# Mixer block: later turns for solves, bonus products and transposes, some elementwise work moved from GpSimd to VectorE, memory values in two bank pairs, no zeroing products

## The chip, the cores and the metric

The program runs on one core of a Trainium2 chip. The metric is the device time of one execution in microseconds (us); of several runs the median counts. The engines are named as in the profile: PE is TensorE (PEld its weight loads), DVE is VectorE, ACT is ScalarE, POOL is GpSimd, SP is SyncE, whose queue issues the DMAs.

## What is computed

Two layers run on 512 positions of width 1024. The first adds a mixer (retention heads beside RWKV-7 heads), a cross-attention over 256 memory rows and an MLP; the second is a gated attention layer. The change touches the mixer and the preparation of the memory keys and values. The parts of the reference that matter:

```python
def wkv7_scan(r, w, k, v, a_vec, b_vec):
    def step(state, inp):
        r_t, w_t, k_t, v_t, a_t, b_t = inp
        sa = jnp.einsum('bhvk,bhk->bhv', state, a_t)
        state = (state * w_t[:, :, None, :] + sa[..., None] * b_t[:, :, None, :]
                 + v_t[..., None] * k_t[:, :, None, :])
        return state, jnp.einsum('bhvk,bhk->bhv', state, r_t)

# in rwkv7_mixer:
    kk = kk / jnp.maximum(jnp.sqrt(jnp.sum(jnp.square(kk), axis=-1, keepdims=True)), 1e-12)
    k = k * (1.0 + (a - 1.0) * k_a)                      # the key update
    y = wkv7_scan(..., -kk, kk * ah)
    bonus = jnp.sum(rh * kh * r_k, axis=-1, keepdims=True) * vh

# in first_block, with memory_cross_attention:
    x = x + y @ w_out[l]
    k, v = jnp.split(rmsnorm(mem, norm_mem[l]) @ w_kv, 2, axis=-1)
```

## The kernel before

**Products in three parts.** A weight unit of 128x1024 is loaded to `raw`, rounded by ACT into a high part `wh` (L291) and subtracted into a low part `wl` (L292, `pump`). A product with an activation is high x high, high x low and low x high (`mm3`, `tile_t`, `quad`). `lowpart` (L246) says which of the 189 units are subtracted on POOL; the others are subtracted on DVE. Units 31 to 54 are the weights of memory keys (31 to 38), memory values (39 to 46) and the mixer's output projection (47 to 54).

**Turns.** PE's instructions run in the order in which the program issues them. `streams` (L616) sets that order: it calls one step of the main generator, counts `now` up by one, and then lets every side generator run whose due time has come. A `yield n` in a side generator means n turns later, a `yield "name"` waits for a flag. One turn of `tile_t` issues four products of 512 columns, one of `tile_n` nine or six of 256 columns, one of `mem_k` eight of 256. Where the main generator itself waits for a flag, turns pass without its products. On the other engines a planner (a model of the timeline that the framework keeps) sets the order, and each then takes its instructions strictly in it.

**The main generator** (`main`, L549) runs, with turn numbers counted from the code: twelve tiles of key, value and receptance for four pairs of heads (turns 1 to 73), the gates (to 83), `ret_g` (to 107), then it needs the flag "products 1", `ret_v` (108 to 132), then it needs "states 0", `ret_k` and `ret_q` (133 to 181), then it needs "mem", `mem_k` (182 to 205) and `mem_v` (206 to 229). After that the mixer's pools are closed and `x1` begins with the output projection.

**The side generators.** `key` (L1426) takes the norm of a key: products `n2`, a reciprocal root on DVE, transposes `rt`, a copy on ACT (L1448), the product `bc` with the constant `indT`, then on DVE and POOL the key update (L1457, L1458) and the rows that need it (L1461). `recept` (L1478) ends with the bonus: L1487 on DVE, some turns later the product `bo` with the constant `bones` (tag "tp") and L1492. `side` (L584) runs once for each half of the heads: `products` fills the 64x64 blocks, `invert` (L1561) inverts their diagonal 32x32 blocks with 62 small POOL instructions and moves them through DRAM, after `self.wait[hf]` turns `solve` (L1601) multiplies the blocks (two halves of 64 very small products), and `chain` (L1620) runs eight chunks of four turns. Half 0: `products` in turns 44 to 56, `solve` in 84 to 88, `chain` in 88 to 120. Half 1: `products` from 80, its last part only after the flag "solve 0", "products 1" at turn 92, `solve` in 114 to 118, `chain` in 120 to 152. Then `mem_norm` (L844, transposes of the two row blocks in turns 159 and 165, the flag "mem" behind the second), `final_rw` (from 160) and, after the flag "q", `ret` (181 to 211).

**In a chunk of the chain** the bank `xy` is first written by a product with a zero tile (`zb`, L1629), then come three of the four products that need no state, the two products with the state `st` of the chunk before (DVE L1656, L1658), and the fourth.

**Banks.** PSUM in the mixer is four pairs of banks, tags "mm", "tp", "cs" and "ch". `psplit` (L871) empties a bank of a result with a copy on ACT (L872) and a subtraction on DVE (L873). `quad` (L906) takes its banks from "mm".

Of the kernel before, what the change touches and what calls it, by code (L numbers as in the profile page):

```python
# [13 lines left out]
ALU = mybir.AluOpType  # L14
AX = mybir.AxisListType

P = 128
S = 512
NB = 4
# [209 lines left out]
class Kern:  # L229
    def __init__(self, ctx, tc, A, out):  # L230
        self.tc, self.nc, self.A, self.out = tc, tc.nc, A, out
        self.T = Ordered(tc, tc.nc.tensor)
        pool = lambda name, **k: ctx.enter_context(tc.tile_pool(name=name, bufs=1, **k))
        self.cp = pool("cp")
        self.wp = pool("wp")
        self.tp = pool("tp")
        self.sp = pool("sp")
        self.sm = pool("sm")
        self.dp = pool("dp", space=bass.MemoryType.DRAM)
        self.nraw = self.nspl = 0  # L240
        self.raw, self.spl = {}, {}
        self.NU = A["wst"].shape[0]
        self.u = 0
        self.cnt = 0
        self.nh = 3
        self.lowpart = lambda u: u <= 3 or 31 <= u < 79 or 145 <= u  # L246
        self.wait = [28, 22]

# [189 lines left out]
    def first(self):  # L438

        nc, A = self.nc, self.A  # L440
        self.zb = self.mp.tile([P, 128], mybir.dt.bfloat16, name="zb")
        nc.gpsimd.memset(self.zb, 0.0)
        xa, xc = self.slab(4, [P, 2, 1024]), self.slab(5, [P, 2, 1024])
# [400 lines left out]
    def mem_norm(self):  # L844
# [3 lines left out]
        for b in range(2):  # L848
# [4 lines left out]
            nc.vector.scalar_tensor_tensor(xs, m, rs, gt, op0=ALU.mult, op1=ALU.mult)  # L853
            yield 6
            self.transp(xs, b, [(mh[0][0][:, 0:4], mh[0][1][:, 0:4]), (mh[0][0][:, 4:8], mh[0][1][:, 4:8])])
# [9 lines left out]
    def mem_v(self):  # L865
        self.mv = (self.slab(0, [P, 2, 1024], F32R), self.slab(1, [P, 2, 1024], F32R))
        for j in range(2):
            c = slice(j * 512, j * 512 + 512)
            yield from self.quad(lambda k: self.mt[k], lambda b, ps: self.psplit((self.mv[0][:, b, c], self.mv[1][:, b, c]), ps), nb=2)

# [34 lines left out]

    def quad(self, act, post, wait=None, outer=False, nb=NB):  # L906

# [3 lines left out]
        for i in range(4):  # L911
# [4 lines left out]
            for j in range(4 if outer else nb):  # L916
                b, q = (i, j) if outer else (j, i)
                if q == 0:
                    ps.append(self.psum("mm"))
                for k in (2 * q, 2 * q + 1):  # L920
# [505 lines left out]
    def key(self, p, sl, ps):  # L1426
# [21 lines left out]
        SC.copy(rts[0:2], rt[0:2].rearrange("p a b -> p (a b)"))  # L1448
        yield 2
        bc = self.psum("tp")  # L1450
# [6 lines left out]
        V.tensor_scalar(u, th, self.hv("k_a", p), self.ka1(p), op0=ALU.mult, op1=ALU.add)  # L1457
        G.tensor_tensor(ks, ks, u, op=ALU.mult)  # L1458
        V.scalar_tensor_tensor(kk, th, 1.0, kk, op0=ALU.add, op1=ALU.mult)
# [18 lines left out]
    def recept(self, p, sl, ps):  # L1478
# [9 lines left out]
        self.flags.add(f"pair {p}")  # L1488
        yield 6
        bo = self.psum("tp")  # L1490
# [129 lines left out]
    def chain(self, hf, sl):  # L1620
# [5 lines left out]
        for c in range(8):  # L1626
            g = gs[c // 4][:, c % 4]
            xy = self.psum("ch", (P, 4, 64))
            self.T.matmul(xy, self.zb, self.zb.unsqueeze(1).broadcast_to([P, 2, 128]), start=True, stop=False)  # L1629
            for h in range(4):  # L1630
                if h == 3 and st is not None:
                    for j in range(2):
                        self.T.matmul(xy[:, 2 * j:2 * j + 2], ar[:, j, c], st[:, j], start=False, stop=False)
                self.T.matmul(xy[0:64, h], g[64:128, h, 0:64], uv[64:128, c, h], start=False, stop=h == 3)
            xs = self.tmp((64, 4, 64), "xs", 1)
# [26 lines left out]
            for h in range(4):  # L1662
                self.T.matmul(xy[64:128, h], g[:, h, 64:128], uv[:, c, h], start=False, stop=h == 3)
            SC.copy(uv[64:128, c], xy[64:128])
# [38 lines left out]
```

## Time and profile before

| | us |
|---|---|
| median of 3 runs | 1331.93 |
| lowest, highest | 1331.39, 1334.37 |
| the profiled execution | 1330.39 |
| its span, first to last instruction | 1328.6 |
| mean granted clock of PE | 0.976 |
| busy share: PE, PEld | 95%, 79% |
| busy share: DVE, ACT, POOL | 53%, 38%, 40% |

The profile's page gives busy time by engine, the span in slices, the chain of work that ended last and groups of instructions by line. A busy share is a mean over stages with different limits, so the stage in which an instruction lies has to be looked at by itself. "Granted clock" is the share of PE's full 2.4 GHz that the chip let through in a stretch: 1.00 is 2.4 GHz, 0.50 is 1.2 GHz. In a row of the timeline the bracket says how long the engine stood idle before the instruction and whose end it then took up.

### The profile page before, as it was taken

What the parts mean: (1) busy time and instruction counts of PE and PEld (TensorE: products, weight loads), DVE (VectorE), ACT (ScalarE), POOL (GpSimd) and SP (SyncE); (2) the same over time, 40 slices, a digit from 0 to 9 for tenths busy, and PEclk for the clock granted to TensorE, in tenths of its full rate; (3) what the DMA queues carried; (4) which work ended last, traced back from release to release, by engine and by line L of the source; (5) the groups of instructions that cost most, each with busy time, mean ns of one, the idle gap of its engine ahead of it and who ended that gap; (6) DMA issues with size and microseconds to landing.
All of it is one profiled execution on the core that took longest, in us unless ns stands there. A gap on an engine that the chain in (4) does not pass through costs nothing.

```text
span 1328.6 us, 18213 instructions
## 1 busy us (share of the span) xinstructions
PE 1257.8 (95%) x6988; PEld 1043.1 (79%) x6988; DVE 699.8 (53%) x1465; ACT 507.7 (38%) x899; POOL 536.7 (40%) x544
## 2 busy tenths in 40 slices
PE   4999799998997989998999999999999999999997
PEld 4667577887895888888888888888887888788886
DVE  5667424456495275546333333332779946665355
ACT  5434323333344234433433322332534435554332
POOL 4924545135666553246311111110214563222474
PEclk9989899899999999999999999999999999999999
DMA  5223313211234422313333233333332232122321
GB/s 188 76 62 83 76 53 72 74 56 41 80 113 143 141 64 80 95 49 111 111 95 96 95 95 96 96 100 100 101 114 80 80 111 64 48 64 64 111 80 64
DMA packets 52376, 117.06 MB, mean 88 GB/s; under 512 B 23072, under 2 KB 23712, under 8 KB 52288
## 3 DMA queue, kind: packets, MB, share of 16 engines
q1 hardware_dynamic: 52112, 115.82, 28.6%
q8 instruction: 55, 0.90, 0.3%
q14 instruction: 33, 0.27, 0.1%
q0 software_dynamic: 32, 0.00, 0.0%
q10 hardware_dynamic: 144, 0.07, 0.0%
HBM read 112.46 MB, written 3.41 MB: 87 GB/s over the span
## 4 chain that ended last, share of the span: by engine, by line
PE 78%; POOL 7%; DVE 7%; issue 3%; ACT 2%; DMA 2%; SPq 0%; DVEq 0%; ACTq 0%; POOLq 0%
PE mm L220 64%; PE ch L220 7%; PE tp L220 4%; POOL s L220 3%; PE cs L220 3%; POOL o L1581 1%; DVE sm L362 1%; POOL s L1583 1%; DVE s L873 1%; DVE sm L358 1%; DMA s<-x 1%; DMA s<-dm 1%; POOL wl L220 0%; ACT t L1056 0%; ACT wh L291 0%
## 5 line engine op out<-in xcount | busy, mean ns | idle before, releaser
L220 PE MATMUL mm<-s,wh 128*128 128x512 f32 (+1 forms) x1424 | 422.5, 378 | 0.0
L220 PE MATMUL mm<-wh,s 128*128 128x512 f32 (+1 forms) x1264 | 364.1, 364 | 7.8 <-DVE s L873 7.8
L220 PEld LDWEIGHTS mm<-s,wh 128*128 128x128 f32 x1424 | 259.1, 191 | 53.2 <-issue 9.7
L220 PEld LDWEIGHTS mm<-wh,s 128*128 128x128 f32 x1264 | 231.2, 192 | 47.2 <-DVE s L873 9.6
L220 PE MATMUL mm<-s,wl 128*128 128x512 f32 (+1 forms) x704 | 263.5, 374 | 0.0
L291 ACT CAST wh<-raw 128x1024 fp32r<-128x1024 f32 x151 | 158.6, 1051 | 250.2 <-PE mm L220 220.2
L292 POOL TENSOR_TENSOR wl<-raw,wh 128x1024 fp32r<-128x1024 f32 x75 | 180.5, 2408 | 156.7 <-ACT wh L291 140.5
L220 PE MATMUL mm<-wl,s 128*128 128x512 f32 (+1 forms) x632 | 227.0, 359 | 2.0 <-POOL wl L292 1.7
L292 DVE TENSOR_TENSOR wl<-raw,wh 128x1024 fp32r<-128x1024 f32 x76 | 95.3, 1253 | 120.9 <-ACT wh L291 120.6
L220 PEld LDWEIGHTS mm<-s,wl 128*128 128x128 f32 x704 | 134.2, 191 | 21.3
L220 PEld LDWEIGHTS mm<-wl,s 128*128 128x128 f32 x632 | 121.9, 193 | 19.1 <-POOL wl L292 2.1
L1074 POOL TENSOR_TENSOR t<-t 128x512 f32<-128x512 f32 x32 | 50.0, 1563 | 214.8 <-ACT t L1073 214.8
L220 PE MATMUL mm<-s,whx 128*128 128x512 f32 (+1 forms) x336 | 100.2, 378 | 0.0
L220 PE MATMUL mm<-whx,s 128*128 128x512 f32 (+1 forms) x272 | 86.5, 377 | 0.6 <-DVE s L873 0.6
L347 DVE TENSOR_TENSOR s<-t,s 128x512 fp32r<-128x512 f32 x44 | 38.6, 877 | 69.9 <-ACT s L346 69.9
L292 POOL TENSOR_TENSOR wlx<-raw,whx 128x1024 fp32r<-128x1024 f32 x18 | 43.7, 2426 | 75.0 <-ACT whx L291 75.0
L220 PEld LDWEIGHTS mm<-s,whx 128*128 128x128 f32 x336 | 62.2, 194 | 10.6 <-DVE s L873 0.4
L220 PE MATMUL ch<-s,s 128*64 128x64 f32 (+3 forms) x504 | 65.2, 274 | 2.5 <-DVE s L873 1.8
L938 DVE TENSOR_TENSOR s<-mm,s 128x256 f32<-128x256 f32 x96 | 35.7, 419 | 58.7 <-PE mm L220 58.5
L291 ACT CAST whx<-raw 128x1024 fp32r<-128x1024 f32 x35 | 36.8, 1052 | 70.6 <-PE mm L220 54.4
L220 PE MATMUL mm<-s,wlx 128*128 128x512 f32 (+1 forms) x168 | 63.2, 376 | 0.0
L220 PEld LDWEIGHTS ch<-s,s 128*64 128x64 f32 (+2 forms) x504 | 47.0, 154 | 16.5 <-DVE s L873 3.7
(268 smaller groups left out, 1703.6 us busy)
## 6 DMA issues: line engine op xcount, KB each, us to landing
raw<-wst SPq DMA_DIRECT2D x189, 512.0 KB, 3.6
s<-x SPq DMA_DIRECT2D x8, 512.0 KB, 5.6
s<-rows SPq DMA_DIRECT2D x7, 512.0 KB, 4.0
out<-t SPq DMA_DIRECT2D x8, 256.0 KB, 2.3
t<-mem SPq DMA_DIRECT2D x2, 512.0 KB, 3.9
dm<-s SPq DMA_DIRECT2D x10, 64.0 KB, 2.0
s<-dm SPq DMA_DIRECT2D x2, 256.0 KB, 4.3
s<-dm SPq DMA_DIRECT2D x8, 64.0 KB, 2.5
```

The costliest lines, as they stand in the source:

```text
L220: r = getattr(self.eng, name)(*a, **k)
L291: (SC or nc.scalar).copy(h, r)
L292: (E or (nc.gpsimd if self.lowpart(self.nspl) else nc.vector)).tensor_tensor(l, r, h.bitcast(F32), op=ALU.subtract)
L347: self.nc.vector.tensor_tensor(dst[1], src, dst[0].bitcast(F32), op=ALU.subtract)
L358: V.scalar_tensor_tensor(t, y, h, y, op0=ALU.mult, op1=ALU.mult)
L362: V.scalar_tensor_tensor(y, t, 1.5, y, op0=ALU.add, op1=ALU.mult)
L873: (V or self.nc.vector).tensor_tensor(dst[1], ps, dst[0].bitcast(F32), op=ALU.subtract)
L938: self.nc.vector.tensor_tensor(xs, ps[:, c], xs, op=ALU.add)
L1074: nc.gpsimd.tensor_tensor(q, r, r, op=ALU.mult)
L1581: G.tensor_tensor(tv, w[:, 0:k, s:s + 1].broadcast_to([P, k, n]), m[:, s:s + 1, s + 1:32].broadcast_to([P, k, n]), op=ALU.mult)
L1583: G.tensor_tensor(w[:, 0:k, s + 1:32], w[:, 0:k, s + 1:32], tv, op=ALU.add)
```

## The change

- `lowpart`: units 31 to 54 are subtracted on DVE, not on POOL.
- `self.wait`: `solve` comes 33 and 25 turns behind its `products`, not 28 and 22.
- The zero tile and the product with it are gone. With a state, the two state products come first in a chunk and start the bank; without one, the first of the four products starts it.
- `mem_norm` transposes 9 turns behind each block's scaling, not 6.
- `mem_v` takes the banks of its first half of columns from "mm" and of its second from "cs".
- In `key`, the product `bc` comes 3 turns behind the copy, not 2, and the key update runs on DVE.
- In `recept`, the bonus product comes 9 turns behind, not 6.

```diff
-        self.lowpart = lambda u: u <= 3 or 31 <= u < 79 or 145 <= u
-        self.wait = [28, 22]
+        self.lowpart = lambda u: u <= 3 or 55 <= u < 79 or 145 <= u
+        self.wait = [33, 25]
...
-        self.zb = self.mp.tile([P, 128], mybir.dt.bfloat16, name="zb")
-        nc.gpsimd.memset(self.zb, 0.0)
...
             nc.vector.scalar_tensor_tensor(xs, m, rs, gt, op0=ALU.mult, op1=ALU.mult)
-            yield 6
+            yield 9
...
-            yield from self.quad(lambda k: self.mt[k], lambda b, ps: self.psplit((self.mv[0][:, b, c], self.mv[1][:, b, c]), ps), nb=2)
+            yield from self.quad(lambda k: self.mt[k], lambda b, ps: self.psplit((self.mv[0][:, b, c], self.mv[1][:, b, c]), ps), nb=2, tag=("mm", "cs")[j])
...
-    def quad(self, act, post, wait=None, outer=False, nb=NB):
+    def quad(self, act, post, wait=None, outer=False, nb=NB, tag="mm"):
...
-                    ps.append(self.psum("mm"))
+                    ps.append(self.psum(tag))
...
         SC.copy(rts[0:2], rt[0:2].rearrange("p a b -> p (a b)"))
-        yield 2
+        yield 3
...
-        G.tensor_tensor(ks, ks, u, op=ALU.mult)
+        V.tensor_tensor(ks, ks, u, op=ALU.mult)
...
         self.flags.add(f"pair {p}")
-        yield 6
+        yield 9
...
             xy = self.psum("ch", (P, 4, 64))
-            self.T.matmul(xy, self.zb, self.zb.unsqueeze(1).broadcast_to([P, 2, 128]), start=True, stop=False)
+            if st is not None:
+                for j in range(2):
+                    self.T.matmul(xy[:, 2 * j:2 * j + 2], ar[:, j, c], st[:, j], start=j == 0, stop=False)
             for h in range(4):
-                if h == 3 and st is not None:
-                    for j in range(2):
-                        self.T.matmul(xy[:, 2 * j:2 * j + 2], ar[:, j, c], st[:, j], start=False, stop=False)
-                self.T.matmul(xy[0:64, h], g[64:128, h, 0:64], uv[64:128, c, h], start=False, stop=h == 3)
+                self.T.matmul(xy[0:64, h], g[64:128, h, 0:64], uv[64:128, c, h], start=st is None and h == 0, stop=h == 3)
...
             for h in range(4):
-                self.T.matmul(xy[64:128, h], g[:, h, 64:128], uv[:, c, h], start=False, stop=h == 3)
+                self.T.matmul(xy[64:128, h], g[:, h, 64:128], uv[:, c, h], start=st is None and h == 0, stop=h == 3)
```

## Rows read from the trace of the kernel before

**Rows 1.** Windows, PE alone: stretch, length, busy (records), granted clock, DMA, GB/s
```profile
58.00:92.00 34.00, 28.94 (x113) 0.90 0.20 62
138.00:150.00 12.00, 8.14 (x38) 0.86 0.20 57
150.00:184.00 34.00, 28.57 (x267) 0.80 0.36 78
218.00:252.00 34.00, 31.52 (x330) 0.80 0.39 91
252.00:316.00 64.00, 62.94 (x579) 1.00 0.17 55
316.00:342.00 26.00, 22.57 (x143) 0.93 0.15 47
396.00:436.00 40.00, 32.16 (x147) 0.96 0.54 174
```

**Rows 2.** Chain that ended last, pieces in order of time: start, us, what
```profile
103.81 1.09 PE cs L220 x16
...
431.32 34.75 PE mm L220 x152
```

**Rows 3.** Groups by line, whole span: busy us, mean ns, idle before and releaser
```profile
L292 DVE TENSOR_TENSOR wl<-raw,wh 128x1024 fp32r<-128x1024 f32 x76 | 95.3, 1253 | 120.9 <-ACT wh L291 120.6
...
L1458 POOL TENSOR_TENSOR kt<-kt,t 128x512 f32<-128x512 f32 x4 | 5.9, 1476 | 5.0 <-DVE t L1457 5.0
L1461 DVE TENSOR_TENSOR s<-kt 128x512 f32<-128x512 f32 x4 | 3.0, 760 | 8.2 <-POOL kt L1458 8.2
```

**Rows 4.** Timeline, PE, two bonus products: start, us, engine, line, shapes, idle before
```profile
61.39 1.12 PE L220 MATMUL tp<-t,cst 128*128 128x512 f32 x2 [1.95 <-DVE t L1487]
...
144.89 0.77 PE L220 MATMUL tp<-t,cst 128*128 128x512 f32 x1 [3.86 <-DVE t L1487]
```

**Rows 5.** Timeline around the key product of the second pair
```profile
72.62 0.31 ACT L687 ACTIVATE sin<-s 128x128 f32<-128x128 f32 x1 [0.71 <-POOL s L220]
...
76.78 0.92 PE L220 MATMUL tp<-t,cst 2*128 2x512 f32 x1 [2.55 <-ACT t L1448]
```

**Rows 6.** Timeline, POOL's last inversion step of half 0, PE's first solve product
```profile
152.33 0.23 POOL L1583 TENSOR_TENSOR s<-s,o 128x16 f32<-128x16 f32 x1
...
159.96 1.24 PE L220 MATMUL cs<-s,s 32*32 32x32 f32 x20 [5.19 <-DMA s<-dm]
```

**Rows 7.** Windows, PE alone, behind the second half of solve 0
```profile
172.00:176.00 4.00, 3.75 (x20) 0.59 0.00 0
```

**Rows 8.** Timeline, POOL's first inversion step of half 1, its first solve product
```profile
182.73 0.24 POOL L1581 TENSOR_TENSOR o<-t,t 128x31 f32<-128x31 f32 x1 [30.16 <-DMA t<-dm]
...
227.91 2.31 PE L220 MATMUL cs<-t,s 32*32 32x32 f32 x40 [2.19 <-DMA t<-dm]
```

**Rows 9.** Timeline, heads of two chunks of the chains
```profile
213.44 0.27 PE L220 MATMUL ch<-zb 128*128 128x256 bf16 x1
213.63 0.63 DVE L1658 TENSOR_TENSOR st<-sc,su 64x128 f32<-64x128 f32 x2
213.64 0.56 PE L220 MATMUL ch<-s,s 64*64 64x64 f32 x6
...
284.71 0.71 PE L220 MATMUL ch<-st,s 128*128 128x128 f32 x4 [0.68 <-DVE st L1658]
```

**Rows 10.** Timeline, PE, a retention transpose behind the second memory block's transposes
```profile
329.76 0.66 PE L220 MATMUL tp<-ident,t 128*128 128x128 f32 x2 [2.79 <-DVE s L873]
```

**Rows 11.** Timeline, end of the memory keys, memory values, first output projection
```profile
398.17 2.35 POOL L292 TENSOR_TENSOR wl<-raw,wh 128x1024 fp32r<-128x1024 f32 x1 [0.78 <-ACT wh L291]
...
398.58 1.97 DVE L1678 TENSOR_SCALAR sm<-sm 128x8 f32<-128x8 f32 x1
...
418.72 0.50 PE L220 MATMUL mm<-wh,s 128*128 128x512 f32 x1 [2.08 <-DVE s L873]
...
431.32 0.50 PE L220 MATMUL mm<-wh,s 128*128 128x512 f32 x1 [1.40 <-DVE s L873]
```

## The prediction

> **What bounds the kernel now.** PE does: in the page's shares it is busy 95% of the span, and most of the chain that ended last is its own products. What can be won is its idle time and the time at the low clock. I read the windows first, for PE alone. In each row the length less the busy time is stall, and the length times (1 less the granted clock) is what the low clock took [rows 1]. Six stretches, all in the mixer, hold nearly all of it: 58 to 92 (stall 5.1, clock 3.4), 138 to 150 (3.9, 1.7), 150 to 184 (5.4, 6.8), 218 to 252 (2.5, 6.8), 316 to 342 (3.4, 1.8) and 396 to 436 (7.8, 1.6), together 28.1 of stall and 22.1 of clock, 50 us. Between them there is next to nothing: 252 to 316 has a stall of 1.1 and the full clock. Then I read the timeline for what ended each stall [rows 4, 5, 6, 8, 10, 11]. The reader is to see that each is one waiting product, and that the clock falls behind it: a stall costs twice. One fall has almost no stall ahead of it: behind the second half of solve 0 the clock is 0.59 over four us in which PE stood for 0.25 [rows 7], so very small products alone bring it down.
>
> **The price of a turn.** 152 products of 512 columns took 34.75 us, 0.229 each, so a turn of four is 0.91 us; a step of sixteen block products is 1.09 [rows 2]. Moving a step later is worth as many turns as lie between, up to its whole stall.
>
> **The change part by part** (the sum against the profiled execution's 1330.39).
>
> *Bonus three turns later, key update on VectorE.* Two of the four bonus products stall, 1.95 and 3.86 us, for L1487 on DVE [rows 4]. Three turns are 2.74. The first stall goes. Of the second 1.1 remains if L1487 is no earlier, none if it gains by the other edit: DVE stood 8.2 us in four waits for POOL's update (1.48 mean), and the same form is 0.76 on DVE [rows 3]. I take 1.1, and that with so short a stall the 1.7 of clock in 138 to 150 goes too: the stall of 1.95 was followed by none. Gain there 2.7 + 1.7 = 4.4. L1492 is queued three turns later on DVE and its bank of "tp" is held until then; the next taker of "tp" comes three turns behind it, for which L1492 must not be late by more than 2.7 us.
>
> *The key product one turn later.* It stalls 2.55 for the copy L1448, which ACT runs behind the sine, and the sine waited 0.71 for POOL's chain of angles [rows 5]. With the 1.95 gone and 0.56 of a smaller wait in the same stretch (5.06 - 1.95 - 2.55), PE arrives 2.51 earlier, less 0.91 for the extra turn: 1.6 earlier. The copy can come earlier only by what POOL saves. Bounds: 0.71, the wait that the row shows, and 1.48, the update that leaves POOL's queue; I take 1.3. So the stall moves here and is 2.55 + 1.6 - 1.3 = 2.85, and its clock loss stays. Gain of the stretch 5.06 - 2.85 = 2.2; if the planner puts the copy ahead of the sine, 5 to 8.
>
> *Solve 0 five turns later.* PE stood 5.19 for the inverted blocks [rows 6]. Its way there grows by five turns, 4.6, and by two block product steps of half 1 that now lie ahead, 2.2; it shrinks by the 4.4 just won. The blocks come 1.3 earlier, since POOL's last update of 1.48 stood in the inversion's queue. Left: 5.2 - 6.8 + 4.4 - 1.3 = 1.5; bounds 0 and 4. The clock: each half of a solve costs one fall as in [rows 7], 4 x 0.41 = 1.6, twice 3.3 instead of 6.8; bounds 1.6 and 6.8. Gain 5.4 - 1.5 + 3.5 = 7.4. All that hangs on it moves too: four copies on ACT, the chain of half 0 with its state scalings on POOL, the last part of half 1's products and "products 1" (turn 97; main asks for it at 107), "states 0" (125; asked for at 132). Main waits at neither. SP is passed by nothing: a solve issues no DMA, and the loads of memory rows that reuse its buffer are wanted only from turn 159.
>
> The rule that speaks against the moved update: VectorE now reads two SBUF operands beside POOL's inversion. In the trace a DVE instruction that begins inside a POOL subtraction of 2.35 takes 1.97 [rows 11]. The Trainium skill, "SBUF — State Buffer", section "SBUF: two separate sides", says that the two engines' shared port pair is locked whole, for the length of whichever instruction came first. By it the update's 0.76 is taken from POOL's inversion again, and the sum would be 0.8 smaller.
>
> *Solve 1.* POOL's inversion of half 1 begins at 182.73, having waited 30 us for a DMA, and the solve stalls 2.19 at 227.91 [rows 8]. That DMA follows the last block products of half 1 (turn 86), which stood behind solve 0 and now come before it, some 20 us earlier. So the blocks are there long before turn 122, where solve 1 now stands, and the stall goes whatever the eight turns do. Left: 0.3 of stall and two clock falls, 3.3; gain 9.3 - 3.6 = 5.7. The chain of half 1 moves by six turns, `mem_norm` with it.
>
> *No zeroing product.* PE goes on 0.20 us after it [rows 9], sixteen times 3.2. But the state product now heads the chunk, and three products that covered it are behind it, with the whole of PE's queue: main's next turn and ACT's copy for the second step. In the late chunks (DVE done at 214.26 where the chunk begins at 213.44, [rows 9]; four such in the two chains) PE loses the cover, 0.20 and about 0.5: 2.8. Net 0.4; bounds 3.2 (none late) and 3.2 - 14 x 0.7 = -6.6 (all that have a state late).
>
> *Memory transposes three turns later.* The second block's transposes take both "tp" banks in a turn in which a retention transpose wants one: 2.79 [rows 10]; 0.64 more was the wait for the scaling (3.43 - 2.79), which three turns (about 3 us here) cover. By the turn count the blocks now come in turns 168 and 177, and retention transposes stand in both, so the collision may happen twice. Bounds +3.4 and -3.5; I take 0. "mem" is set at 177, main asks at 182, five turns of about one us; before there were seventeen. Nothing waits unless the split on DVE is late by more.
>
> *Two bank pairs, 24 units on VectorE.* The second half of memory values waits 2.08 for a bank of the first half, and the output projection 1.40 for one of the second [rows 11]; with "cs" both go: 3.5. The other two, 7.84 - 2.08 - 1.40 = 4.4, are waits for L873 on DVE, behind a small instruction that POOL's subtraction stretched to 1.97; now a subtraction of 1.25 [rows 3] stands in DVE's own queue. Between 0 and 4.4, I take 1.0, and half the clock loss, 0.8. Gain 5.3. DVE's load: 24 x 1.25 = 30 us more over some 110, against what POOL's 24 x 2.4 held it up. In its strict queue each subtraction waits for ACT's high part, with splits behind it, and the next tile's banks wait for these.
>
> *What I can't see.* The planner will order ACT, DVE and POOL anew. Stretches without a known cause lose 1.1 in 64 us; over the mixer's 400, and as the stalls moved, 0 to 8. I take 3 against.
>
> **Sum:** 2.2 + 4.4 + 7.4 + 5.7 + 0.4 + 0 + 5.3 - 3 = 22.4. The profiled execution would be 1308.0. The median of the runs is 1.5 above the profiled one, so 1331.93 - 22.4 = 1309.5.
>
> **The rivals.**
> 1. *The solves hold the clock down.* The stalls go, but the very small products keep PE at 1.2 GHz as long as now, and solve 0 still waits 3 to 4. For: the fall in [rows 7]. Against: that fall took 1.6 of the stretch's 6.8, the longer part came behind the stall. Price 3.5 + 3.5 + 2 = 9, and as much again if the state products come late in most chunks: 1318 to 1326, middle 1320. Chance 0.18.
> 2. *Cleaner than thought.* The key copy is put ahead, solve 0 waits for nothing, values stand for nothing: 5 + 1.5 + 3 + 3, and no new stalls, 3: 1309.5 - 15.5 = 1294. Chance 0.13.
> 3. *VectorE becomes the bound* (slower). In memory keys and values a subtraction at the head of DVE's queue waits for ACT's high part while a full bank waits behind it, and PE stands some 2 per unit, as DVE stood behind POOL [rows 11]. It decides once DVE is more than two units behind PE. For: its strict queue, and retention norms in the same stretch. Against: POOL's subtraction, which it replaces, held DVE longer. Over sixteen units 32 us: 1309.5 + 32 = 1341; from twelve units on the whole gain is gone. Chance 0.06.
> 4. *The change doesn't do what it says:* the stalls only move, as at the key product, and each later wait takes what an earlier one gave: 1331. Chance 0.05.
>
> **How the numbers follow.** Forecast 0.58 (own range 1301 to 1317), rivals 0.18, 0.13, 0.06, 0.05. Predicted 1309.5. The range runs from 1292, below the middle of rival 2, to 1323, above that of rival 1; left out are rivals 3 and 4 and the ends of 1 and 2, about 0.18. A difference of 0.2% (2.7 us) is about what a measurement can tell from none. Faster: 0.58 + 0.18 + 0.13 = 0.89; same 0.05; slower 0.06.
>
> **What would show it.** The windows of the mixer: no stall at the second, third and fourth bonus products over 1.1, about 2.9 at the second key product, under 2 at solve 0, none at solve 1, with POOL's second inversion beginning some 20 us sooner; none at the second half of values and at the output projection. Wrong if solve 0 or the key product stall over 4, if the clock in the solves' stretches stays under 0.85, or if PE waits for `wl` or L873 in memory keys. Behind the mixer the two traces should run alike.

## The result, and the profile after

| | before | after |
|---|---|---|
| median, us | 1332.66 (4 runs) | 1315.58 (4 runs) |
| lowest, highest | 1331.39, 1334.37 | 1313.71, 1317.52 |
| the profiled execution, its span | 1330.39, 1328.6 | 1317.52, 1315.7 |
| mean granted clock | 0.976 | 0.981 |
| first output projection, second half of values emptied | 431.32 | 416.63 |
| from there to the end of the span | 897.3 | 899.1 |

The ratio is 0.9881, with a 95% interval of 0.9859 to 0.9903: 17 us faster, where 22.4 were predicted. The time lies in the range, six above the forecast. The last two rows say where to look: all of the gain stands ahead of the output projection, and behind it the two traces run alike to 1.8 us. The profiled execution of after is the slowest of its four, so the two profiles differ by 12.9 where the medians differ by 17, and the ratio gives 16.

Line numbers of after are two or three lower than before's: L1586 are the copies of the inverted blocks, L1446 the key's copy, L871 the split's subtraction, L1538 the mask of the block products, L1655 the chain's state.

Windows of after, PE alone, cut at the stages of [rows 1] (length, busy, records, granted clock, DMA, GB/s):

```profile
58.00:92.00 34.00, 29.93 (x131) 0.90 0.21 62
138.00:147.00 9.00, 8.92 (x58) 1.00 0.43 118
147.00:182.00 35.00, 27.52 (x275) 0.90 0.40 91
182.00:216.00 34.00, 30.54 (x256) 1.00 0.30 70
216.00:250.00 34.00, 32.94 (x410) 1.00 0.26 82
250.00:303.00 53.00, 50.29 (x438) 0.90 0.16 52
303.00:336.00 33.00, 29.79 (x210) 1.00 0.12 39
336.00:392.00 56.00, 52.68 (x455) 0.97 0.35 101
392.00:418.00 26.00, 21.67 (x99) 1.00 0.59 191
```

Timeline of after, PE: the products that waited, and the three that waited before and don't now (142.78 the fourth bonus, 163.83 solve 0, 227.30 solve 1):

```profile
76.24 1.71 PE L220 MATMUL tp<-t,cst 2*128 2x512 f32 x2 [4.06 <-ACT t L1446]
142.78 1.02 PE L220 MATMUL tp<-t,cst 128*128 128x512 f32 x2
154.48 2.67 PE L220 MATMUL cs<-s,s 64*128 64x128 f32 x16 [7.56 <-DVE s L1538]
163.83 2.21 PE L220 MATMUL cs<-s,s 32*32 32x32 f32 x64
202.63 0.68 PE L220 MATMUL ch<-st,s 128*128 128x128 f32 x4 [1.27 <-DVE gs L1675]
227.30 2.21 PE L220 MATMUL cs<-t,s 32*32 32x32 f32 x64
274.18 0.79 PE L220 MATMUL ch<-st,s 128*128 128x128 f32 x4 [2.02 <-DVE gs L353]
349.51 1.93 PE L220 MATMUL cs<-s,s 64*128 64x128 f32 x14 [3.06 <-DVE t L836]
402.76 0.66 PE L220 MATMUL tp<-ident,t 128*128 128x128 f32 x4 [2.93 <-POOL t L1685]
416.63 0.50 PE L220 MATMUL mm<-wh,s 128*128 128x512 f32 x1 [1.40 <-DVE s L871]
```

Stall and clock loss of each stage, worked out as in the prediction (length less busy; length times 1 less the clock), beside what was predicted for it:

| stage | before | after | gain | predicted |
|---|---|---|---|---|
| first bonus, key product | 5.1 + 3.4 | 4.1 + 3.4 | 1.0 | 2.2 |
| fourth bonus | 3.9 + 1.7 | 0.1 + 0 | 5.5 | 4.4 |
| solve 0 | 5.4 + 6.8 | 7.5 + 3.5 | 1.2 | 7.4 |
| solve 1 | 2.5 + 6.8 | 1.1 + 0 | 8.2 | 5.7 |
| the stretches between, to the retention | 1.2 + 0 | 6.2 + 5.3 | -10.3 | -3 - 2.8 |
| memory transposes | 3.4 + 1.8 | 3.2 + 0 | 2.0 | 0 |
| retention, memory keys | 0 + 0 | 3.3 + 1.7 | -5.0 | 0 |
| memory values, output projection | 7.8 + 1.6 | 4.3 + 0 | 5.1 | 5.3 |
| sixteen zeroing products | 3.2 | 0 | 3.2 | 3.2 |

They add up to 10.9 of the 14.7 us by which the projection comes sooner; the clock term is rough, since it counts idle time at the low clock twice, and each column is one execution, while the same stall can cost more or less of the clock in another (last section). The 0.4 predicted for the zeroing products stands here as its two parts, 3.2 and the 2.8 of late states. The transposes did collide twice, as the prediction feared, but for 1.50 and 1.05, where one collision and the scaling had cost 3.43. The reader is to see three things: most of the named stalls went as foretold; solve 0 gave little; and stretches that had no stall lost 15.

**Solve 0.** PE no longer waits for the inverted blocks, but for the third block product step of half 1, which now lies ahead of the solve. The timeline of after from POOL's last inversion step to DVE's mask:

```profile
149.72 0.23 POOL L1581 TENSOR_TENSOR s<-s,o 128x16 f32<-128x16 f32 x1
...
149.98 2.14 ACT L1586 COPY s<-s 32x512 f32<-32x512 f32 x2 [9.64 <-POOL s L1581]
152.14 0.63 ACT L1500 ACTIVATE kt<-t 128x512 f32<-128x512 f32 x1
...
152.81 0.43 DVE L1501 TENSOR_SCALAR kt<-kt 128x512 f32<-128x512 f32 x1 [9.80 <-ACT kt L1500]
...
153.75 1.28 DVE L1538 TENSOR_TENSOR s<-cs,cst 128x512 f32<-128x512 f32 x2
```

ACT stands at the copies of half 0's blocks for 9.64 us, because the planner put them ahead of the gate's tanh (L1500); behind the tanh stands DVE, and behind DVE the banks "cs" that the third step needs. The queue was the same before: there ACT's copies stood 10.13, until POOL's step of [rows 6]. But the third step lay behind solve 0, which waited for the same inversion in any case. Timeline of before, ACT:

```profile
152.60 2.26 ACT L1588 COPY s<-s 32x512 f32<-32x512 f32 x2 [10.13 <-POOL s L1583]
```

**The key product** has the same form: ACT's sine waited for POOL's angles, with the key's copy L1446 behind it. **Solve 1** went for the reason foretold, though by less: POOL's second inversion begins 12.7 sooner than in [rows 8], not 20. Timeline of after, the sine on ACT and POOL's second inversion:

```profile
71.13 0.31 ACT L685 ACTIVATE sin<-s 128x128 f32<-128x128 f32 x1 [7.02 <-POOL s L220]
...
170.03 0.24 POOL L1579 TENSOR_TENSOR o<-t,t 128x31 f32<-128x31 f32 x1 [20.08 <-DMA t<-dm]
```

### The profile page after: what moved, and what is told of

The parts are those of the page before. It is cut to its first block, busy times and chain, and to the rows that moved or that the text cites. A ratio compares the mean times of both kernels' runs of the same rounds, so it can differ in the third digit from the quotient of the medians.

```text
span 1315.7 us, 18199 instructions
## 1 busy us (share of the span) xinstructions
PE 1244.0 (95%) x6972; PEld 1036.2 (79%) x6972; DVE 708.0 (54%) x1493; ACT 507.0 (39%) x899; POOL 472.7 (36%) x515
## 4 chain that ended last, share of the span: by engine, by line
PE 61%; DVE 5%; ACT 2%; issue 1%; POOL 1%; DMA 0%; DVEq 0%; ACTq 0%; POOLq 0%
PE mm L220 54%; PE ch L220 3%; PE tp L220 3%; DVE sm L362 1%; DVE sm L358 1%; PE cs L220 1%; DVE s L871 1%; ACT t L1054 0%; DVE t L1056 0%; ACT wh L291 0%; DMA raw<-wst 0%; DVE sm L1051 0%; DVE t L1117 0%; DVE s L1333 0%; POOL wlx L292 0%
## 5 line engine op out<-in xcount | busy, mean ns | idle before, releaser
L220 PE MATMUL mm<-wh,s 128*128 128x512 f32 (+1 forms) x1232 | 351.0, 361 | 2.4 <-DVE s L871 1.4
L220 PEld LDWEIGHTS mm<-wh,s 128*128 128x128 f32 x1232 | 223.0, 191 | 38.4 <-DVE s L871 1.8
L220 PE MATMUL mm<-wl,s 128*128 128x512 f32 (+1 forms) x616 | 219.4, 356 | 1.8 <-POOL wl L292 1.8
L292 DVE TENSOR_TENSOR wl<-raw,wh 128x1024 fp32r<-128x1024 f32 x99 | 123.7, 1249 | 166.5 <-ACT wh L291 164.0
L292 POOL TENSOR_TENSOR wl<-raw,wh 128x1024 fp32r<-128x1024 f32 x52 | 125.5, 2416 | 133.3 <-ACT wh L291 122.1
L220 PEld LDWEIGHTS mm<-wl,s 128*128 128x128 f32 x616 | 117.5, 191 | 18.2 <-POOL wl L292 2.2
L347 DVE TENSOR_TENSOR s<-t,s 128x512 fp32r<-128x512 f32 x44 | 34.8, 791 | 65.4 <-ACT s L346 65.4
L955 POOL TENSOR_TENSOR t<-s,s 128x256 f32<-128x256 f32 x48 | 34.2, 739 | 70.9 <-DVE s L936 57.6
```

The source lines that it names most:

```text
L220: r = getattr(self.eng, name)(*a, **k)
L292: (E or (nc.gpsimd if self.lowpart(self.nspl) else nc.vector)).tensor_tensor(l, r, h.bitcast(F32), op=ALU.subtract)
L347: self.nc.vector.tensor_tensor(dst[1], src, dst[0].bitcast(F32), op=ALU.subtract)
L955: nc.gpsimd.tensor_tensor(st[b][1][:, c], x[:, c], st["g"][:, c], op=ALU.mult)
```

## The experiments

**Theory:** the front half of the gain (bonus, key, solves) is eaten by strict queues, above all ACT's, which hold PE until POOL's inversion ends whatever PE won before; the last stage carries the rest. **Rivals:** the waits of the solves are the gain, as the prediction had it; or the lost part went to the state products that now head a chunk. Ratios are to the kernel before on the same chip, whose medians there lie between 1328.51 and 1332.66, so that ratios and medians can differ by some us; where that matters, both are given. The last column is the start of the first output projection in the one execution that was profiled.

| kernel | median | ratio, 95% interval | projection |
|---|---|---|---|
| before | 1332.66 | 1 | 431.32 |
| after | 1315.58 | 0.9881 (0.9859 to 0.9903) | 416.63 |
| after, zeroing product back | 1315.23 | 0.9899 (0.9873 to 0.9924) | 414.36 |
| after, copies on POOL | 1312.87 | 0.9881 (0.9855 to 0.9908) | 413.48 |
| after, solves' waits back | 1314.86 | 0.9892 (0.9865 to 0.9919) | 414.90 |
| after, key update back | 1317.52 | 0.9907 (0.9880 to 0.9934) | 418.37 |
| after, bonus and key delays back | 1316.82 | 0.9892 (0.9873 to 0.9911) | 415.84 |
| after, sines late | 1313.86 | 0.9862 (0.9840 to 0.9885) | 410.18 |
| after, copies late on ACT | 1322.51 | 0.9934 (0.9913 to 0.9955) | 422.24 |
| after, one bank pair | 1316.30 | 0.9887 (0.9868 to 0.9905) | 415.92 |
| after, 24 units on POOL | 1322.61 | 0.9963 (0.9942 to 0.9985) | 422.24 |
| before, last stage's edits alone | 1317.78 | 0.9924 (0.9899 to 0.9948) | 415.06 |
| after, sines late, copies on POOL, waits 36 and 22 | 1298.23 | 0.9786 (0.9760 to 0.9812) | 399.06 |
| the same, more of the order set | 1295.53 | 0.9763 (0.9734 to 0.9792) | 398.32 |

**The solves' waits back.**

```diff
-        self.wait = [33, 25]
+        self.wait = [28, 22]
```

> The changed kernel with the solves 28 and 22 turns behind, as before. Theory (the prediction's step for solve 0, corrected): solve 0 stands ahead of the third block product step again and waits for blocks that land some 7.4 us behind the inversion's end of 149.95, at 157.4, where PE now goes on at 154.48: 3 of stall more and up to 3.4 of clock; solve 1's blocks are there long before, so its three turns are worth nothing: 3 to 6 slower than the changed kernel, 1319 to 1322. Rival (the waits are the main part of the gain, as the prediction had it, 13.1 for both solves): 8 or more slower, over 1323. Rival (the change of solves moves nothing): 1316.

The last answer came: 1314.86, no difference. Timeline of that kernel: solve 0, a product of the chain with the rows of ACT ahead of it, and two products of the retention.

```profile
156.45 0.76 PE L220 MATMUL cs<-s,s 32*32 32x32 f32 x11 [10.63 <-DMA s<-dm]
...
214.20 2.14 ACT L1586 COPY t<-t 32x512 f32<-32x512 f32 x2 [3.00 <-POOL t L1581]
216.37 0.36 ACT L1639 COPY s<-ch 64x256 f32<-64x256 f32 x1
216.78 0.92 PE L220 MATMUL ch<-s,s 128*64 128x64 f32 x16 [2.18 <-ACT s L1639]
...
346.59 0.60 PE L220 MATMUL cs<-s,s 64*128 64x128 f32 x6 [1.12 <-DVE t L836]
...
396.48 0.66 PE L220 MATMUL tp<-ident,t 128*128 128x128 f32 x4 [0.92 <-POOL t L1685]
```

Solve 0 waits 10.63 and the clock is 0.50 in 150 to 160, worse than with the new waits. But half 1 ends its chain six turns sooner, and the two stalls of the retention, 3.06 and 2.93 in the changed kernel, are 1.12 and 0.92: 3.9 come back there, less a new wait of 0.93 (391.14). Solve 1 waits for no block here either, but the 2.19 of [rows 8] have only changed their name: ACT stands 3.00 for the second inversion at the copies of half 1's blocks, with the chain's copy L1639 behind them, and PE waits 2.18 for that. POOL's second inversion begins at 179.15 here, 9.1 later than with the new waits, where the same queue costs PE 0.84 (ACT's copy L1633, the product at 206.75). So the new waits did shorten both waits, 10.63 to 7.56 and 2.18 to 0.84, and the retention took most of it back.

**Bonus and key delays back, key update back.** Two kernels:

```diff
-        yield 3
+        yield 2
         bc = self.psum("tp")
...
         self.flags.add(f"pair {p}")
-        yield 9
+        yield 6
```

> The changed kernel with the bonus products 6 turns behind and the key product 2, as before. Theory (what PE wins ahead of the third block product step of half 1 is eaten there): that step goes on when POOL's inversion of half 0 ends, 149.72 plus 4.8 in the changed kernel, whatever PE did before. So the bonus stalls come back (up to 1.95 near 61, up to 3 near 143), the wait of 7.56 shrinks by the later ones, and the whole is within 2 us of the changed kernel, 1315 to 1318. Rival (the prediction's sum, 2.2 + 4.4 for these stretches): 6 or more slower, over 1321.

```diff
-        V.tensor_tensor(ks, ks, u, op=ALU.mult)
+        G.tensor_tensor(ks, ks, u, op=ALU.mult)
```

> The changed kernel with the key update back on POOL. Theory (the prediction's step): POOL's inversion of half 0 ends 1.3 to 1.5 later and with it the 7.56 us wait, and DVE's rows for the second and fourth bonus come up to 2.7 later, for which 1.1 of stall may come back: 1.5 to 3 slower, 1317 to 1319. Rival: VectorE gains nothing by the move, since VectorE and POOL hold each other up in the same stretch: 1315 to 1316.

1316.82 and 1317.52. With the old delays no bonus product waits at all: the update on DVE is enough for both stalls; the key product waits 4.79, and the third step 6.90, until 155.91. With the update on POOL the bonus doesn't wait either (that is the delays' work), but DVE stands in its queue for POOL, and PE waits for DVE's L525:

```profile
146.02 1.22 PE L220 MATMUL mm<-s,wh 128*128 128x512 f32 x2 [3.20 <-DVE t L525]
```

The third step waits only 1.31 there, until 161.35: POOL's inversion ends 4.9 later, mostly because it begins 4.5 later, and PE is late as well. So the two edits remove the same stalls, and each is worth little beside the other; the update's 1.9 by the medians and 3.5 by the ratios are not told from none.

**The zeroing product back**, with three products ahead of the state again.

```diff
...
-            if st is not None:
-                for j in range(2):
-                    self.T.matmul(xy[:, 2 * j:2 * j + 2], ar[:, j, c], st[:, j], start=j == 0, stop=False)
+            self.T.matmul(xy, self.zb, self.zb.unsqueeze(1).broadcast_to([P, 2, 128]), start=True, stop=False)
             for h in range(4):
+                if h == 3 and st is not None:
+                    for j in range(2):
+                        self.T.matmul(xy[:, 2 * j:2 * j + 2], ar[:, j, c], st[:, j], start=False, stop=False)
...
```

> The changed kernel with the zeroing product back and the state products again behind three others. In the changed kernel's trace three state products head a chunk and come late (1.27, 0.20 and 2.02 us of idle PE), and behind the last the granted clock is 0.50 to 0.65 from 274 to 284, about 5 us. Theory (the cover was worth more than the product): sixteen products of 0.20 cost 3.2, some 2.5 of stall and 5 of clock come back, so about 4 faster than the changed kernel, near 1311. Rival (the late states come from the queue order on DVE, not from the place in the chunk): the stalls stay, and it is 3 slower, near 1319.

1315.23: between the two, not told from none. The late states of 1.27 and 2.02 shrink to 0.47 and 1.31, so the cover was worth 1.5 of stall, and the product costs 3.2. Behind the 1.31 the clock stays at 1.00; behind the 2.02 of the changed kernel it is 0.53 over ten us, which most other runs with the same 2.02 show less of (last section). So the edit is worth nothing that can be measured, as the prediction's 0.4 had it, and what a late state costs in clock, 0 to 4.7, weighs more than its wait.

**One bank pair for the values.**

```diff
-... nb=2, tag=("mm", "cs")[j])
+... nb=2, tag="mm")
```

> The changed kernel with both halves of the memory values in the banks of mm, as before. Theory (the prediction's step): the second half and the output projection wait for banks again, 2.08 and 1.40 in the kernel before; the 1.40 stands in the changed kernel too, so 2 to 3 come back at the second half: 1317 to 1319. Rival (without POOL's subtractions DVE empties the banks in time, so that the second pair is worth nothing): within 1 us of the changed kernel.

The rival: 1316.30, and no wait at the second half. The output projection's 1.40, which the second pair was to remove as well, stands in every kernel here, whichever banks the second half has: PE takes up the end of the last subtraction of the values (L871, until 416.58 in the changed kernel). The mixer's banks are given up there; whether that is why, no run shows.

**The 24 units on POOL.**

```diff
-        self.lowpart = lambda u: u <= 3 or 55 <= u < 79 or 145 <= u
+        self.lowpart = lambda u: u <= 3 or 31 <= u < 79 or 145 <= u
```

> The changed kernel with the low parts of units 31 to 54 on POOL again. The run with both halves of the values in one pair of banks showed no wait at the second half, so that pair is worth nothing beside this edit. Theory (the 24 units carry the whole gain of the last stage): with POOL's subtractions of 2.35 back, PE waits for the low part's banks (L871) in keys and values as before, 4.4 of it at the least, of the 2.93 at the retention transpose (402.76) none or more: 3 to 6 slower than the changed kernel, 1319 to 1322. Rival (the stage is held by the retention norms on DVE, not by POOL): within 1.5 us of the changed kernel.

1322.61, 7.0 by the medians and 10.9 by the ratios (0.0082 of 1330, some 4 either way): the one part whose undoing shows plainly. Timeline of that kernel:

```profile
350.44 0.80 PE L220 MATMUL cs<-s,s 64*128 64x128 f32 x4 [4.15 <-DVE t L836]
...
374.65 2.39 POOL L292 TENSOR_TENSOR wl<-raw,wh 128x1024 fp32r<-128x1024 f32 x1 [3.72 <-ACT wh L291]
...
374.79 2.29 DVE L353 TENSOR_SCALAR sm<-sm 128x8 int32<-128x8 int32 x1
...
378.09 0.50 PE L220 MATMUL mm<-s,wh 128*128 128x256 f32 x2 [1.22 <-DVE s L871]
```

A DVE instruction on eight columns, 0.17 elsewhere, takes 2.29 where it begins inside POOL's subtraction, and PE waits for the split behind it. The Trainium skill, "SBUF — State Buffer", section "SBUF: two separate sides", has the port pair that the two engines share locked for a whole instruction, by whichever of them starts first. The rows agree: DVE's instruction ends at 377.08, POOL's at 377.04. POOL's own queue suffers as well: rotary steps and the add L831 stand behind subtractions of 2.4, and PE's wait for L836 is 4.15, not 3.06.

**The last stage's edits alone**, on the kernel before: the 24 units, the two bank pairs, the transposes nine turns behind.

```diff
-        self.lowpart = lambda u: u <= 3 or 31 <= u < 79 or 145 <= u
+        self.lowpart = lambda u: u <= 3 or 55 <= u < 79 or 145 <= u
...
-            yield 6
+            yield 9
...
-... nb=2)
+... nb=2, tag=("mm", "cs")[j])
...
```

> The kernel before with the last stage's edits alone: low parts of units 31 to 54 on DVE, values in two bank pairs, memory transposes 9 turns behind. The edits ahead of it (waits, bonus and key delays, key update, zeroing product) are as before. Undone one by one in the changed kernel, those four were worth -0.4 to +2 us each, the 24 units 7. Theory (the front edits are worth something together that none is worth alone, since each undone stall is taken by the wait next to it): the back edits give 5 to 8 here, 1323 to 1327, and the front edits the other 8 to 11. Rival (the front edits are worth what they are singly, 3 in sum): 1316 to 1319.

1317.78, where the rival stood by the median; the ratio lies between it and the theory. Timeline of that kernel, PE: the old stalls stand, the retention's are small.

```profile
141.34 1.22 PE L220 MATMUL tp<-t,cst 128*128 128x512 f32 x1 [3.86 <-DVE t L1487]
...
156.40 0.81 PE L220 MATMUL cs<-s,s 32*32 32x32 f32 x12 [5.34 <-DMA s<-dm]
...
222.18 1.02 PE L220 MATMUL cs<-t,s 32*32 32x32 f32 x23 [1.98 <-DMA t<-dm]
```

By the ratios these edits give 10 us (0.0076 of 1330, 7 to 13) and the front edits the other 5.7 (some 4 either way; by the medians, 2.2). The run before says the same from the other side: without the 24 units, 4.9 are left (0.0037 of 1330, 2.0 to 7.7). The profiles can't settle it finer: here the projection comes at 415.06, 1.6 sooner than in the changed kernel, but the profiled execution is the fastest of eleven here and the slowest of four there. Of its lead of 16.3 over before, some 7.5 are stalls and clock of the memory stages, and most of the rest, about 7, is less low clock behind front stalls that are much the same as before's. In the stretch of solve 0 it is 0.85 here (147 to 181), in that of solve 1 it is 0.90, where [rows 1] have 0.80 for both:

```profile
214.00:247.00 33.00, 30.73 (x350) 0.90 0.47 112
```

**ACT's queue at the key product.** ACT may take the sines only behind the square of the third key; the order is set by a dependency between instructions of one engine.

```diff
-        for x, o in ((acc, self.sin), (w, self.cos)):
+        for x in (acc, w):
             V.tensor_scalar(x, x, -0.4999999, 0.4999999, op0=ALU.max, op1=ALU.min)
-            nc.scalar.activation(o, x, AF.Sin, scale=2.0 * math.pi)
+        yield 75
+        for x, o in ((acc, self.sin), (w, self.cos)):
+            self.after(nc.scalar.activation(o, x, AF.Sin, scale=2.0 * math.pi), "square")
...
```

> The changed kernel with one thing more: ACT may take the sine and cosine (L685) only behind the square of the third pair's key, some 20 us later. Theory: the 4.06 us at the key product (76.24) are ACT standing 7.02 us in its strict queue for POOL's angles, not the product's turn: with the sines behind, that stall goes, with its 1.7 to 3.4 of low clock, the inversion starts that much earlier, and the kernel is 4 to 7 faster than the changed one, 1308 to 1311. Rival (the banks of tp or the norm's other steps hold the product): the stall stays over 2, within 2 us of the changed kernel.

The stall at the key product and its low clock are gone (the clock is 1.00 from 70 to 90), and the projection comes at 410.18, 6.5 sooner than in the changed kernel. By the median the run is 1.7 faster, by the ratio 2.5, which is not told from none; its executions lie from 1310.21 to 1316.20, and the profiled one, 1310.70, is near the fastest. So the cause of the stall is shown, and what it is worth by itself isn't. The window of the key product in that kernel, and the third step:

```profile
70.00:80.00 10.00, 10.00 (x46) 1.00 0.21 53
```

```profile
149.73 0.58 PE L220 MATMUL cs<-s,s 64*128 64x128 f32 x1 [7.73 <-DVE s L1544]
```

PE's lead arrives at the third step, which still waits 7.73: what is won ahead of it moves the whole on only because the inversion ends 6.0 sooner as well (143.68 for 149.72). The move has a price there: ACT loads a table for 1.28 between the copies and the gate's tanh (146.09), which it doesn't in the changed kernel.

**ACT's queue at solve 0**, in two ways: the copies on POOL, or on ACT behind the gate.

```diff
-            SC.copy(m[o, :, 0:16], w[o].rearrange("p i t -> p t i"))
+            G.tensor_copy(m[o, :, 0:16], w[o].rearrange("p i t -> p t i"))
```

> The changed kernel with the two copies of the inverted blocks (L1586) on POOL, not on ACT. Theory: the 7.56 us of idle PE at 154.48 stand on ACT's strict queue: the copies waited there 9.64 us for POOL's inversion, with the gate's activation L1500 behind them, behind that DVE L1538, and behind that the banks of the third block product step. With the copies on POOL this wait is gone, PE comes to solve 0 some 8 earlier and waits there 1 to 4 for the blocks, of the low clock 0 to 3.4 goes: 4 to 8 faster than the changed kernel, 1308 to 1312. Rival: the wait only moves to solve 0, whose blocks come no earlier: within 1 us of the changed kernel.

```diff
...
+        self.spawn(self.inv_out(hf, sl, m, w, half), 32 if hf == 0 else 0)
...
-            SC.copy(m[o, :, 0:16], w[o].rearrange("p i t -> p t i"))
+            self.after(SC.copy(m[o, :, 0:16], w[o].rearrange("p i t -> p t i")), "gate")
...
```

> The changed kernel with one thing more: ACT may take the copies of the inverted blocks (L1586) only behind the second gate's tanh (L1500). Theory: no wait at the third block product step (7.56 in the changed kernel); PE comes to solve 0 some 8 us sooner and waits there 2 to 5 for the blocks, which land some 7.5 behind the inversion's end, near 157.5, where solve 0 began at 163.83: 4 to 7 faster, 1309 to 1312. Against the run with the copies on POOL (blocks at 159.73) 2 faster. Rival: the wait only moves to solve 0, and the low clock behind it takes the rest: within 1.5 us of the changed kernel.

In both the third step waits for nothing, so the queue is its cause. In both the wait goes to solve 0, and there it is longer than I expected: 6.59 and 11.92. The first kernel is 2.7 faster by the median and not by the ratio, the second 7 slower. The timeline of the second, its copies done at 152.6 (SPq is the queue on which SP issues DMAs):

```profile
153.86 1.93 SPq L1606 DMA_DIRECT2D s<-dm  x4
155.89 0.96 SPq L1550 DMA_DIRECT2D dm<-s  x2
156.90 0.50 SPq L287 DMA_DIRECT2D raw<-wst  x1
157.44 1.33 SPq L1598 DMA_DIRECT2D dm<-s  x2
162.59 0.31 SPq L1602 DMA_DIRECT2D s<-dm  x1
...
165.23 3.59 PE L220 MATMUL cs<-s,s 32*32 32x32 f32 x64 [11.92 <-DMA s<-dm]
```

My edit issues the blocks' DMAs later, so SP's own strict queue has them (L1598) behind four reads, two writes of half 1 and a weight load: five us after the copies they start. With the copies on POOL it is the same in small, one of the two writes stands behind a read (L1595, 153.94), and the read that solve 0 needs (L1591) behind three more:

```profile
154.32 0.58 SPq L1587 DMA_DIRECT2D dm<-s  x1
154.96 1.72 SPq L1595 DMA_DIRECT2D s<-dm  x3
156.92 0.30 SPq L1591 DMA_DIRECT2D s<-dm  x1
```

**All of it together.** Sines late, copies on POOL with the read that solve 0 needs (L1591) set ahead of the four that it doesn't, and the waits at 36 and 22:

```diff
-        self.wait = [33, 25]
+        self.wait = [36, 22]
...
-        nc.sync.dma_start(sv, d1.rearrange("p t c -> t p c"))
+        self.mark["sv"] = nc.sync.dma_start(sv, d1.rearrange("p t c -> t p c")).ins
...
-                nc.sync.dma_start(gs[q]...)
+                self.after(nc.sync.dma_start(gs[q]...), "sv")
...
```

> The changed kernel with three things: the sines on ACT behind the square of the third key, the copies of the inverted blocks on POOL (with the DMA that solve 0 needs ahead of the four that it doesn't), and the waits 36 and 22. Theory (the lost gain stands in ACT's strict queue): the sine run alone gave 6.5 us up to the output projection; here the third block product step waits for nothing either, and solve 0 waits 0 to 2 where it waited 6.59 with the copies on POOL alone: 11 to 15 faster than the changed kernel, 1301 to 1305. Rival (the blocks' landing holds solve 0 whatever else moves): as the sine run, 1309 to 1312.

1298.23, a ratio of 0.9786 (0.9760 to 0.9812), better than both kernels and beyond the theory's 1301 to 1305. The third step waits 1.86, solve 0 for nothing, and the projection comes 17.6 sooner than in the changed kernel. The third step:

```profile
149.15 1.09 PE L220 MATMUL cs<-s,s 64*128 64x128 f32 x6 [1.86 <-DVE s L1544]
```

No step tried alone did it: the sines' lead, which stood at the third step, and the copies' lead, which stood at solve 0, seem to be paid out together. The reads' order and the waits of 36 and 22 weren't run by themselves, so how the gain divides is not shown. The run with more of the order set on DVE:

```diff
...
+        self.after(V.tensor_reduce(mu, y, axis=AX.X, op=ALU.add), "state")
...
+            if e is nc.vector:
+                self.after(r, "state")
...
-            G.tensor_tensor(t, t, self.bv[:, p], op=ALU.add)
+            V.tensor_tensor(t, t, self.bv[:, p], op=ALU.add)
...
             self.gnorm(y, 8, 1e-5, yn, yn, ("pt", 2))
-            yield 9
+            yield 12
```

> The run before (sines, copies on POOL, waits 36 and 22) with more: on DVE the first reduction of a chunk's norm and each subtraction of a weight unit come behind the last state of the chain that was issued; the add L831 on DVE, not POOL; the retention's transposes 12 turns behind the norm, not 9. Theory: the late states (1.27, 0.20, 2.02), half of the 3.06 at L836 and the 2.93 at the retention transpose go: 4 to 6 faster than the run before, 1296 to 1301. Rival (weight units late behind the states, so that PE waits for wl): no faster than the run before.

1295.53, a ratio of 0.9763 (0.9734 to 0.9792): the interval overlaps that of the run before, and its projection is only 0.7 sooner. The retention's wait falls from 2.88 to 1.14 and L836's from 2.19 to 1.37; one late state stays at 1.89, and solve 0 waits 1.37 again.

## Why the prediction was right in its number and wrong in its working

**Right.** PE bounds the kernel, the six stretches hold the loss, and the gain ends at the output projection. The bonus stalls went, the fourth with its low clock (5.5 for 4.4). Solve 1's stall went for the reason given, the earlier last block products, and its low clock went altogether (8.2 for 5.7); but 6.8 of clock was much for a stall of 2.2, the kernel with the last stage alone loses 3.3 behind 1.98. The moved update did shorten POOL's inversion, by 0.9 (35.1 from 117.20 to 152.33 before, 34.2 from 115.48 to 149.72 after), where I took 1.3 and the rule would leave 0.5; with the update alone put back it is 34.6, so that 0.4 of the 0.9 is seen to be its own. VectorE didn't become the bound: PE never waits for `wl` in the memory stages.

**Wrong, solve 0: 7.4 predicted, 1.2 found.** The failed step is "its way there grows by two block product steps of half 1 that now lie ahead, 2.2". I counted these steps as cover. They need banks that DVE empties behind ACT, and ACT waits for the inversion just as the solve does. The row was in the trace of before, in ACT's queue: the same copies, the same wait. I asked who waits for the solve and not what stands behind the copies. In the kernel with everything set in order the third step waits 1.86 and solve 0 for nothing.

**Wrong, the key product: 2.2 predicted, 1.0 found.** The mis-sized term was "I take 1.3" for how much sooner the copy comes: the product began 0.5 sooner (76.24 for 76.78) and stalled 4.06, not 2.85.

**Wrong, the unseen: 3 predicted, and 2.8 for late states, 15 found** in the stage table. Late states (1.27 and 2.02, where I allowed four of 0.7), waits for ACT's copies in the chain (1.05 and 0.84), the low clock behind the 2.02, and in the retention two stalls of 3, of which the solves' later turns brought two thirds: with the old waits they are 1.12 and 0.92. The edit that I credited with most of 13.1 gives back what it takes.

**Wrong, the last stage: 5.3 predicted, 10 found** by the ratios, with the transposes, which I put at 0. "Between 0 and 4.4, I take 1.0" was the mis-sized term, and the 2.08 for the second bank pair was put down to the wrong edit: with the 24 units on DVE, one pair is enough. The 1.40 at the output projection was counted as won ("with "cs" both go") and stayed. I priced what POOL's subtractions did to the waits for L873 and left out POOL's own queue and the small DVE steps of the norms, each of which a subtraction can stretch from 0.17 to over 2.

**So the sum came out near by luck, by errors against each other:** the front edits were put at 20.1 (2.2 + 4.4 + 7.4 + 5.7 + 0.4) and are worth about 5, the last stage at 5.3 and is worth about 10, with 3 taken off for what can't be seen. Rival 4, "each later wait takes what an earlier one gave", with a chance of 0.05, is what the front half did; it was set up for the whole kernel, so that it couldn't be right for one half. Of my signs, "under 2 at solve 0" held in the letter and missed the point, "wrong if the key product stalls over 4" was met, by 0.06, and "none at the output projection" failed, by 1.40.

**Open.** How the front edits' 5 divide: each undone alone costs 1.5 to 3.5 us by the ratios, with some 4 either way. The transposes nine turns behind were not undone alone.

## What to carry to other kernels

Before a wait is covered with other work, follow that work's banks and operands back through each in-order queue: if one of them passes the instruction that the wait is for, the stall only changes its name. Where a planner orders queues, look for long idle times on the engines that aren't the bound (ACT stood 7.02 and 9.64 us) and ask what is queued behind; setting the order of some instructions and DMA issues, with two copies on another engine and new waits, gave 13 us more by the ratios and 17 by the medians, about as much as the whole change. And undo parts from both ends: singly, most edits here looked worthless; the one that didn't, and half of the edits alone on the kernel before, agree on which half carried the gain.

## What the runs showed of the hardware

**Very small products don't bring the clock down by themselves.** The prediction took that from [rows 7], 0.59 behind a stall of 0.25. In the changed kernel both solves, 128 such products each, run at the full 2.4 GHz, with no stall directly ahead of them; in the kernel with the last stage alone solve 1 follows a wait of 1.98, and the clock is 0.57. In that kernel the very place of [rows 7], with the same stall of 0.25 behind the second half of solve 0, stays at 1.00. The windows of after, and behind them two of that kernel:

```profile
163.00:172.00 9.00, 9.00 (x148) 1.00 0.52 134
226.00:236.00 10.00, 10.00 (x178) 1.00 0.47 145
274.00:284.00 10.00, 9.82 (x58) 0.53 0.18 52
```

```profile
168.00:172.00 4.00, 3.75 (x29) 1.00 0.06 9
222.00:230.00 8.00, 7.82 (x95) 0.57 0.30 73
```

With the solves' waits back, the same place falls again, to 0.50 (171 to 173): what decides it there is not shown.

**What a stall costs in clock is not fixed.** The third row above is what followed the state's wait of 2.02: 4.7 us lost in ten. The same product with the same wait of 2.02 stands in seven other kernels. With the late copies it is followed by 0.52 over ten us; in the six others, the one with the copies on POOL among them, by 0.83, a loss of 1.7:

```profile
271.00:281.00 10.00, 9.68 (x81) 0.83 0.17 52
```

So a term of two or three us per stall, as the prediction used, holds as a mean over stalls at best, and executions of one kernel differ by more: those of before lie from 1322 to 1335 over the comparisons.
